# Four plain tiles and one block product in the first third of a feed-forward layer, instead of six plain tiles

## The chip, the cores and the metric

The kernel runs on one core of one Trainium2 chip. The metric is the device time of one execution in microseconds. It is given as the median of three runs. One more execution was taken with the hardware profiler, and its time is given beside its span.

## The reference, cut to what matters

One decoder layer in float32 on 512 tokens of width 1024: a SwiGLU feed-forward at half weight, a mixer (state-space heads and differential attention), cross-attention into 256 memory positions, a second feed-forward and a last norm. The change lies in the first feed-forward alone:

```
def swiglu(h, w_in, w_out):
    gate, up = jnp.split(h @ w_in, 2, axis=-1)
    return (jax.nn.silu(gate) * up) @ w_out

x = x + 0.5 * swiglu(rms_norm(x, norm_ffn1_w[l]), ffn1_w_in[l], ffn1_w_out[l])
```

`w_in` is 1024 x 5632 and `w_out` is 2816 x 1024. The 2816 inner columns are 22 tiles of 128.

## The kernel before, in words

**Precision.** A float32 product is made of three products of rounded parts: each operand is split into a high part (h) and the rest (l), and hh, hl and lh are added. A weight tile of 128 x 1024 is loaded raw (`wr`), ScalarE makes its high part (`wh`), and VectorE the low part (`wl`), lines 155 and 156. There are six buffers for `wr` and three each for `wh` and `wl`.

**Tiles of the first feed-forward** (`ffn1`). The 22 inner tiles are worked in thirds of 6, 8 and 8 (`THIRDS`). In each third the tiles come first, and then `out_blocks` multiplies them with their part of `w_out` and adds the result to x. A tile can be made in two ways.

- **Plain** (`proj`): gate (`pg`) and up (`pu`) each take 8 blocks of the inner dimension times 3 products, that is 24 matmuls 128x512. `gated` turns the two into the tile `th`: VectorE multiplies `pg` by the row of the norm (line 426), ScalarE applies silu (427), and VectorE multiplies with `pu` into `th` (429, 430, 432).
- **By blocks** (`quad`): two tiles at once by the scheme of Strassen and Winograd, which has seven block products instead of eight. Each block product is 24 matmuls 128x256 (line 240). The seven go, in this order, into `qa` (block 11), `qe` (S1), `qb` (S2), `qa` (12), `qb` (S3), `qe` (S4), `qb` (22). Each needs its own weights: five blocks or sums of blocks are loaded, two of the sums are added up by the DMA queue of GpSimd (line 248), and two more by VectorE (lines 294 and 297). ScalarE copies `qa` into `qb` between the first and the third product (line 289).

The block scheme needs sums of blocks of its input: `block_sums` makes them from x, in four pairs of rows, as S1 to S4 in the parts `s31h`, `s31l`, `s24h` and `s24l` (each pair: `fe`, `fo`, four rows 128x256 and two low parts on VectorE). They are used by all block products of the first feed-forward.

**Before**, `NPLAIN` is 6: the first third is made of six plain tiles. The first two (`ffn_first`, tiles `pa`) use weights that arrive with x. The other four are a loop of four steps, and the block sums are made beside it: pairs 0 and 1 in its first step, pair 2 in its second, pair 3 in its third. The second and third thirds have four `quad`s each.

**Accumulators.** Plain tiles, block products and half of the accumulators of `out_blocks` draw from one pool of four PSUM buffers (`accp`), in turn: a fifth tile takes the buffer of the first, when the last reader of the first is done.

**What sets the order.** SyncE and GpSimd issue in the order in which the program is written (`manual_schedule`). Code that runs beside a dense stage is put in by a small planner (`Order`), which counts TensorE's time in microseconds. On TensorE, VectorE and ScalarE a list scheduler puts the instructions in order when the kernel is built, by its own estimate of when inputs are there. On the chip each engine works down its list in order, so an instruction that is not ready holds up all that stand behind it.

**x by token.** `out_blocks` updates x by token, so `by_token` (line 495) loads x again in the other layout into the same buffers, in eight loads on GpSimd's queue, once the block sums have read the old contents. `out_blocks` asks for its first weights ahead of time (`next(out)`), and the sums of its blocks are added up on GpSimd's queue (line 1316 before) or by VectorE (1326, 1367). Its accumulators are `oa`, `oe` and `ob`, and line 1307 adds them to x.

Of the kernel before, what the change touches and what calls it, by code (L numbers as in the profile page):

```python
# [22 lines left out]
MEM = 256  # L23
EPS = 1e-6

NPLAIN = 6

THIRDS = ((0, 6), (6, 8), (14, 8))
THIRDS2 = ((0, 6), (6, 8), (14, 8))
# [71 lines left out]
def body(tc, a, dbg=None):  # L101
# [17 lines left out]
    def s2(s, dt=F32, shape=(P, T)):  # L119
        if math.prod(shape[1:]) <= T // 2:  # L120
            return sp.tile(list(shape), dt, tag="s1", name=nm(s), bufs=NHALF)
        return sp.tile(list(shape), dt, tag="s2", name=nm(s))

    def s4(s):
        return sp.tile([P, 4, T // 2], F32, tag=s, name=nm(s), bufs=1)

    def small(s, n, bufs=None):
        return tiny.tile([P, n], F32, tag=s, name=nm(s), bufs=bufs)

    def acc(s, shape=(P, T)):  # L130
        return acc_p.tile(list(shape), F32, tag="acc", name=nm(s))
# [10 lines left out]
    od = Order()  # L142
# [29 lines left out]
    def load_w(src, n=D):  # L172
        raw = wp.tile([P, n], F32, tag="wr", name=nm("wr"), bufs=6)
        nc.sync.dma_start(raw, src)
        hi = wp.tile([P, n], R32, tag="wh", name=nm("wh"))
        lo = wp.tile([P, n], R32, tag="wl", name=nm("wl"))
        with ExitStack() as after:
            for i in start:
                after.enter_context(tc.issue_after(i))
            recent[:] = [i.ins for i in split_into(hi, lo, raw)]  # L180
        return hi, lo

    @contextmanager
    def behind(ins):
        with ExitStack() as after:
            for i in ins:
                after.enter_context(tc.issue_after(i))
            yield
# [29 lines left out]
    def block_sums(k0, gain, blocks):  # L218

        fe, fo = s2("fe"), s2("fo")  # L220
        V.tensor_scalar(fe, x[k0], par[:, gain + k0 : gain + k0 + 1], None, ALU.mult)
        V.tensor_scalar(fo, x[k0 + 1], par[:, gain + k0 + 1 : gain + k0 + 2], None, ALU.mult)
        return blocks | sums_of(fe[:, :H], fe[:, H:], fo[:, H:], fo[:, :H])

    def of_halves(even, odd):
        lo, hi = slice(0, H), slice(H, T)
        return {"11": hl(even, lo), "12": hl(odd, lo), "22": hl(odd, hi)}
# [90 lines left out]
    def proj(ps, w, xs, ks=None):  # L318
        n = len(xs)
        for k in ks or range(n):  # L320
            mm3(ps, w, xs[k], k == 0, k == n - 1, wc=slice(k * P, (k + 1) * P))
            yield
# [101 lines left out]
    def gated(pg, pu, row, th, odd):  # L424
        gate = s2("gate")
        V.tensor_tensor(gate, pg, row, ALU.mult)
        S.activation(gate, gate, AF.Silu)
        if odd:
            V.tensor_tensor(th[:, 3], pu[:, :H], gate[:, :H], ALU.mult)
            V.tensor_tensor(th[:, 2], pu[:, H:], gate[:, H:], ALU.mult)  # L430
        else:
            V.tensor_tensor(th[:, 0:2], halves(pu), halves(gate), ALU.mult)

    def ffn_quads(xs, wq, st, nq, made, places, sums=None, fresh=False, prime=None):

        for q in range(nq):
            for out in quad(xs, next(wq), next(sums) if sums else None, fresh and q == 0):
                if out is None:
                    yield
            gs, us = out  # L440
            if prime and q == nq - 1:
                next(prime)
            gate, th = s4("gate"), s4("th")
            for i in range(2):
                row = st.row[:, None, i * H : (i + 1) * H].to_broadcast([P, 2, H])
                V.tensor_tensor(gate[:, 2 * i : 2 * i + 2], halves(gs[i]), row, ALU.mult)
            S.activation(gate, gate, AF.Silu)
            for i in range(2):
                V.tensor_tensor(th[:, places[i]], halves(us[i]), gate[:, 2 * i : 2 * i + 2], ALU.mult)
            made(th)  # L450
            yield
# [3 lines left out]
    def block_tiles(g, n, tied=False):  # L455
        def steps(th, blocks, apart):
            b11 = [s2("g11" + p_, R32, (P, H)) for p_ in "hl"]
            split_into(*b11, th[:, 0])
            blocks["11"] = tuple(b11)
            yield apart  # L460
            for sums in sums_in_steps(*(th[:, i] for i in range(4)), pair=(th[:, 0:2], th[:, 1:3])):
                blocks |= sums or {}
                yield apart
            raw = split("g", th[:, 2:4].rearrange("p a b -> p (a b)"))
            lo, hi = slice(0, H), slice(H, T)
            blocks |= {"22": hl(raw, lo), "12": hl(raw, hi)}

        def made(th):
            g.append({})
            if len(g) < n:  # L470
                od.spawn(steps(th, g[-1], 2.9), 2.9)
            else:
                with behind(list(recent) if tied else []):
                    for _ in steps(th, g[-1], 0.0):
                        pass
        return made

    def ffn_first(h, wa):

        ps = [acc("pa"), aux("pa"), acc("pa"), aux("pa")]  # L480
        for k in range(KT):
            for n in range(4):
                mm3(ps[n], wa[k], h[k], k == 0, k == KT - 1, wc=slice(n * P, (n + 1) * P))
            yield
        yield ps[0], ps[2]
        yield ps[1], ps[3]

    def ffn1(h, wa, at_out, each, done):
        xs = []
        wq, plain = iter(a["f1q"]), a["f1i"]  # L490
        col4, ncol4 = small("col4", 4, bufs=1), small("ncol4", 4, bufs=1)

        def by_token():
            for k in (6, 7, 0, 1, 4, 5, 2, 3):
                G.dma_start(x[k], a["xt"][k])
                yield 0.5

        for ti, (_, nf) in enumerate(THIRDS):
            g = []
            nq = nf // 2  # L500
            made = block_tiles(g, nq, True)
            out = out_blocks(a[f"f1b{ti}"], None, g, col4, ncol4, each if ti == len(THIRDS) - 1 else None, n=nq)
            if ti == 0:
                th, f = s4("th"), 0
                for ps in ffn_first(h, wa):
                    if ps is None:
                        yield
                    else:
                        gated(*ps, st1.row, th, f)
                        f += 1  # L510
                made(th)
                V.tensor_scalar(col4, st1.col, 0.5, None, ALU.mult)
                V.tensor_scalar(ncol4, st1.col, -0.5, None, ALU.mult)
                for n in range(NPLAIN - 2):
                    for i in ((0, 1), (2,), (3,), ())[n]:
                        blocks = of_halves(h[2 * i], h[2 * i + 1])
                        b11 = tuple(s2("h11" + p_, R32, (P, H)) for p_ in "hl")
                        with behind(start):
                            for to, of in zip(b11, blocks["11"]):
                                S.activation(to, of.bitcast(F32), AF.Copy)  # L520
                        xs.append(block_sums(2 * i, C_FFN1, blocks | {"11": b11}))
                    if n == 3:
                        od.spawn(by_token())
                    pg, pu = acc("pg"), acc("pu")
                    yield from proj(pg, load_w(plain[n][0]), h)
                    yield from proj(pu, load_w(plain[n][1]), h)
                    if n % 2 == 0:
                        th = s4("th")
                    if n == NPLAIN - 3:
                        next(out)  # L530
                    gated(pg, pu, st1.row, th, n % 2)
                    if n % 2:
                        made(th)
                h.clear()
                nq -= NPLAIN // 2
            yield from ffn_quads(xs, wq, st1, nq, made, BY_BLOCK, prime=out)
            at_out(ti)
            if ti == len(THIRDS) - 1:
                xs.clear()
            yield from out  # L540
        done()
        banks = [acc, aux, acc, aux]
        yield from turn(1, banks)
        yield from turn(0, banks)
# [923 lines left out]
def layout(i):  # L1468
# [12 lines left out]
    for n, s in (("1", "ffn1"), ("2", "ffn2")):  # L1481
        wi = tiles(i[f"{s}_w_in"][0]).reshape(2 * NF, P, KT // 2, 2, P)
        f0 = NPLAIN if n == "1" else 0

# [5 lines left out]
        if n == "1":  # L1490
            d["f1i"] = wi.reshape(2, NF, P, D)[:, 2:NPLAIN].swapaxes(0, 1).copy()
        wo = i[f"{s}_w_out"][0]
# [48 lines left out]
```

## Time and profile before

| | |
|---|---|
| median of three runs | 1319.59 us (1316.08, 1319.59, 1319.67) |
| profiled execution | 1317.81 us |
| its span (first to last instruction) | 1315.9 us |
| TensorE matmul busy | 1289.6 us, 98% |
| VectorE busy | 984.2 us, 75% |
| ScalarE busy | 706.4 us, 54% |
| GpSimd busy | 129.2 us, 10% |
| granted TensorE clock, mean | 0.997 |

A row of the timeline has the start in us from the span's start, how long it took, the engine and the line, what is written and read, and in brackets how long the engine had been idle before it and what ended that. Matmuls are pipelined, so a row's duration is longer than the distance from one start to the next; the distance is what they cost. The same holds for VectorE, to a smaller extent. PE stands for TensorE, DVE for VectorE, ACT for ScalarE, POOL for GpSimd and SP for SyncE.

### The profile page before, as it was taken

What the parts mean: (1) busy time and instruction counts of PE and PEld (TensorE: products, weight loads), DVE (VectorE), ACT (ScalarE), POOL (GpSimd) and SP (SyncE); (2) the same over time, 40 slices, a digit from 0 to 9 for tenths busy, and PEclk for the clock granted to TensorE, in tenths of its full rate; (3) what the DMA queues carried; (4) which work ended last, traced back from release to release, by engine and by line L of the source; (5) the groups of instructions that cost most, each with busy time, mean ns of one, the idle gap of its engine ahead of it and who ended that gap; (6) DMA issues with size and microseconds to landing.
All of it is one profiled execution on the core that took longest, in us unless ns stands there. A gap on an engine that the chain in (4) does not pass through costs nothing.

```text
span 1315.9 us, 20140 instructions
## 1 busy us (share of the span) xinstructions
PE 1289.6 (98%) x7724; PEld 1124.8 (85%) x7724; DVE 984.2 (75%) x1564; ACT 706.4 (54%) x1192; POOL 129.2 (10%) x151
## 2 busy tenths in 40 slices
PE   9999999999999999999999999999999999999996
PEld 7889998998887778777788877888889999989995
DVE  7987888788775676557867786645678878877786
ACT  6544564565754464346645465434465646555564
POOL 0201001001010011111003022020001000000001
PEclk9999999999999999999999999999999999999998
DMA  7377768776994434763465548683239775556652
GB/s 274 120 192 190 205 183 218 217 200 168 285 294 145 135 67 124 255 178 105 93 187 175 170 132 241 193 224 123 66 101 268 211 231 187 182 192 186 193 195 81
DMA packets 69615, 236.33 MB, mean 180 GB/s; under 512 B 8256, under 2 KB 9760, under 8 KB 69168
## 3 DMA queue, kind: packets, MB, share of 16 engines
q1 hardware_dynamic: 53200, 181.11, 40.2%
q0 software_dynamic: 13520, 46.72, 19.2%
q10 hardware_dynamic: 2800, 7.23, 1.6%
q8 instruction: 60, 0.98, 0.3%
q14 instruction: 35, 0.29, 0.1%
HBM read 232.87 MB, written 50.91 MB: 216 GB/s over the span
## 4 chain that ended last, share of the span: by engine, by line
PE 57%; issue 11%; DVE 4%; ACT 2%; POOL 1%; DMA 1%; POOLq 0%; ACTq 0%; DVEq 0%
PE pm L146 10%; PE qb L240 8%; PE qe L240 5%; PE pxbc L146 5%; PE qa L240 5%; PE pcq L146 3%; PE pz L146 3%; PE ob L1296 3%; PE oa L1296 2%; PE oe L1296 2%; PE pq L146 2%; PE pcv L146 1%; PE pv L146 1%; PE pk L146 1%; DVE wl L156 1%
## 5 line engine op out<-in xcount | busy, mean ns | idle before, releaser
L155 ACT ACTIVATE wh<-wr 128x1024 fp32r<-128x1024 f32 (+1 forms) x329 | 334.3, 1019 | 359.8 <-issue 65.1
L156 DVE TENSOR_TENSOR wl<-wr,wh 128x1024 fp32r<-128x1024 f32 (+1 forms) x329 | 385.5, 1175 | 141.3 <-ACT wh L155 138.3
L774 ACT ACTIVATE ec<-ec,mn 128x512 f32<-128x512 f32 (+3 forms) x64 | 35.4, 554 | 33.8 <-DVE mn L773 33.7
L146 PE MATMUL pxbc<-hnh,wh 128*128 128x512 f32 x128 | 52.6, 411 | 0.0
L146 PE MATMUL pxbc<-hnh,wl 128*128 128x512 f32 x128 | 50.3, 393 | 0.0
L146 PE MATMUL pxbc<-hnl,wh 128*128 128x512 f32 x128 | 50.2, 392 | 0.0
L240 PE MATMUL qb<-s31h,wh 128*128 128x256 f32 x152 | 43.2, 284 | 3.2 <-ACT u L299 3.2
L240 PE MATMUL qe<-s31h,wl 128*128 128x256 f32 x152 | 43.2, 284 | 0.6 <-DVE wl L156 0.6
L240 PE MATMUL qb<-s24h,wl 128*128 128x256 f32 x152 | 43.1, 284 | 0.5 <-DVE wl L156 0.5
L240 PE MATMUL qa<-h11h,wh 128*128 128x256 f32 x152 | 43.1, 283 | 0.0
L240 PE MATMUL qe<-s24h,wl 128*128 128x256 f32 x152 | 43.0, 283 | 0.0
L240 PE MATMUL qb<-hmh,wh 128*128 128x256 f32 x152 | 43.0, 283 | 0.0
L240 PE MATMUL qb<-hmh,wl 128*128 128x256 f32 x152 | 43.0, 283 | 0.0
L240 PE MATMUL qe<-s24l,wh 128*128 128x256 f32 x152 | 43.0, 283 | 0.0
L240 PE MATMUL qe<-s24h,wh 128*128 128x256 f32 x152 | 43.0, 283 | 0.0
L240 PE MATMUL qa<-h11h,wl 128*128 128x256 f32 x152 | 43.0, 283 | 0.0
L240 PE MATMUL qa<-hmh,wh 128*128 128x256 f32 x152 | 43.0, 283 | 0.0
L240 PE MATMUL qa<-hml,wh 128*128 128x256 f32 x152 | 43.0, 283 | 0.0
L240 PE MATMUL qb<-hml,wh 128*128 128x256 f32 x152 | 43.0, 283 | 0.0
L240 PE MATMUL qb<-s24h,wh 128*128 128x256 f32 x152 | 43.0, 283 | 0.0
L240 PE MATMUL qa<-h11l,wh 128*128 128x256 f32 x152 | 43.0, 283 | 0.0
L240 PE MATMUL qb<-s24l,wh 128*128 128x256 f32 x152 | 43.0, 283 | 0.0
(449 smaller groups left out, 4173.6 us busy)
## 6 DMA issues: line engine op xcount, KB each, us to landing
wr<-in_f2q SPq DMA_DIRECT2D x44, 512.0 KB, 4.5
wr<-in_f1q SPq DMA_DIRECT2D x40, 512.0 KB, 4.2
wr<-in_f1b SPq DMA_DIRECT2D x30, 512.0 KB, 4.5
isum<-in_f2q SPq DMA_DIRECT2D x22, 512.0 KB, 6.0
wr<-isum SPq DMA_DIRECT2D x22, 512.0 KB, 4.2
wsum<-in_f2b SPq DMA_DIRECT2D x20, 512.0 KB, 6.7
wr<-wsum SPq DMA_DIRECT2D x20, 512.0 KB, 4.4
wr<-in_f1q POOLq DMA_DIRECT2D x16, 512.0 KB, 5.9
```

Source lines behind the costliest of these rows:

```text
L146: newest_mm[:] = [nc.tensor.matmul(out, w, x, start=start, stop=stop).ins]
L155: S.activation(hi, src, AF.Copy),
L156: V.tensor_tensor(lo, src, hi.bitcast(F32), ALU.subtract),
L240: newest_mm[:] = [nc.tensor.matmul(out, a_[:, wc], b_, start=first and f == 0 and kp == 0 and j == 0, stop=kp == n - 1 and j == 2, skip_gr ...
L774: S.activation(ec[:, :n], ec[:, :n], AF.Exp, bias=mn, scale=-1.0, accum_out=sm[c][:, i : i + 1])
L1296: newest_mm[:] = [nc.tensor.matmul(ps, a_[:, ts], b_[:, ws], start=first and k == 0 and j == 0, stop=k == n - 1 and j == 2, skip_group_che ...
```

## The change

`NPLAIN` becomes 4. The first third is now two tiles from `ffn_first`, two plain tiles, and one `quad` that makes the fifth and sixth. The loop has two steps, and each makes two pairs of block sums. The loads of x by token are asked for behind the loop. The early request of `out_blocks` (`next(out)`) was in the loop's last step but one; it is now made at the end of the `quad`. The weights of the tiles concerned are laid out as blocks instead of plain tiles.

```
-NPLAIN = 6
+NPLAIN = 4
...
                 for n in range(NPLAIN - 2):
-                    for i in ((0, 1), (2,), (3,), ())[n]:
+                    for i in ((0, 1), (2, 3))[n]:
...
-                    if n == 3:
-                        od.spawn(by_token())
...
-                    if n == NPLAIN - 3:
-                        next(out)
                     gated(pg, pu, st1.row, th, n % 2)
...
                 h.clear()
+                od.spawn(by_token())
                 nq -= NPLAIN // 2
             yield from ffn_quads(xs, wq, st1, nq, made, BY_BLOCK, prime=out)
```

Line numbers behind the change are lower by 3 from `by_token` on. Beyond the first third and its `out_blocks` the order on every engine is as it was, but for one matmul named below. Three places show what moves.

**VectorE, between the first two plain tiles and what follows.** Before, these are the last rows up to the product of `pu` and its gate that ends the reading of the first `pu`. `fe`, `fo` and `s` are block sums, `gl` belongs to the tiles from `ffn_first`; the number behind a name tells one tile from another.

```order
L156 TENSOR_TENSOR wl_700<-wr_697,wh_699 128x1024
L210 TENSOR_TENSOR s_120_555<-s_119_554,fe_550 128x256
L601 TENSOR_REDUCE lsum_934<-lamp_933 128x1
L211 TENSOR_TENSOR s_120_555<-s_120_555,fo_551 128x256
L156 TENSOR_TENSOR s31l_561<-s_119_554,s31h_560 128x512
L156 TENSOR_TENSOR s24l_565<-s_120_555,s24h_564 128x512
L156 TENSOR_TENSOR gl_589<-th_284,gh_588 128x512
L426 TENSOR_TENSOR gate_634<-pg_568,row_405 128x512
L432 TENSOR_TENSOR th_541<-pu_463,gate_542 128x512
```

Now the rows up to the same product are these:

```order
L156 TENSOR_TENSOR wl_749<-wr_663,wh_748 128x1024
L210 TENSOR_TENSOR s_130_577<-s_129_576,fe_572 128x256
L297 TENSOR_TENSOR wr_663<-wr_663,wr_668 128x1024
L211 TENSOR_TENSOR s_130_577<-s_130_577,fo_573 128x256
L156 TENSOR_TENSOR s31l_583<-s_129_576,s31h_582 128x512
L156 TENSOR_TENSOR wl_790<-wr_668,wh_789 128x1024
L156 TENSOR_TENSOR s24l_587<-s_130_577,s24h_586 128x512
L598 TENSOR_REDUCE lsum_1028<-lamp_1027 128x1
L156 TENSOR_TENSOR gl_611<-th_284,gh_610 128x512
L426 TENSOR_TENSOR gate_656<-pg_590,row_405 128x512
L432 TENSOR_TENSOR th_541<-pu_463,gate_542 128x512
```

Between `gate_542`, the gate of the first plain tile, and its product `th_541<-pu_463,gate_542` stood 12 rows before, and there stand 25 now: two pairs of block sums instead of one, and five rows 128x1024 of the quad's weights (three `wl`, and the additions of lines 294 and 297) instead of one.

**TensorE, from the quad's first product to its second.** `pg_462`, `pu_463`, `pg_590`, `pu_591` were the four tiles before it in the pool of four, `qa_673`, `qe_674` and `qb_675` follow, so `qe_674` takes the buffer of `pu_463`.

```order
L240 MATMUL qa_673<-h11h_568,wl_677 128x256
L1343 MATMUL ob_957<-ones_r 128x512
L240 MATMUL qe_674<-s31h_432,wh_680 128x256 [waits DVE_49,Activation_49]
L240 MATMUL qe_674<-s31l_433,wh_680 128x256
L240 MATMUL qe_674<-s31h_432,wl_681 128x256
```

Before, plain matmuls stood here. The count of VectorE's rows for which the first matmul of `qe_674` waits is 95, and the 95th row is `th_541<-pu_463,gate_542`. The matmul from `ones_r` clears an accumulator of `out_blocks`; before it stood at the head of `out_blocks`.

**VectorE, in `out_blocks` of the first third, around the update of x from `oa`.** Before, the low parts of the weights for the next product stand ahead of the update (`wl_1004` is needed by its third matmul):

```order
L156 TENSOR_TENSOR wl_1004<-wr_1000,wh_1003 128x1024
L156 TENSOR_TENSOR wl_1027<-wr_1023,wh_1026 128x512
L1307 SCALAR_TENSOR_TENSOR x_79<-oa_858,col_59_282,x_79 128x512
L1307 SCALAR_TENSOR_TENSOR x_83<-oa_859,col_59_282,x_83 128x512
L156 TENSOR_TENSOR wl_1041<-wr_1038,wh_1040 128x1024
```

Now they stand behind it:

```order
L1304 SCALAR_TENSOR_TENSOR x_79<-oa_952,col_59_282,x_79 128x512
L1304 SCALAR_TENSOR_TENSOR x_83<-oa_953,col_59_282,x_83 128x512
L156 TENSOR_TENSOR wl_1098<-wr_1094,wh_1097 128x1024
L156 TENSOR_TENSOR wl_1121<-wr_1117,wh_1120 128x512
L156 TENSOR_TENSOR wl_1135<-wr_1132,wh_1134 128x1024
```

On TensorE four matmuls of that product which need no `wl` are put first, and then the clearing matmul of the next third, which before stood in the first quad behind:

```order
L1293 MATMUL ob_956<-wh_1097,s31h_515 128x512
L1293 MATMUL ob_956<-wh_1097,s31l_516 128x512
L1293 MATMUL ob_957<-wh_1097,s31h_515 128x512
L1293 MATMUL ob_957<-wh_1097,s31l_516 128x512
L1343 MATMUL ob_2206<-ones_r 128x512
L1293 MATMUL ob_956<-wl_1098,s31h_515 128x512
```

On SyncE the first quad of the second third asks for its second raw tile when `wl_1121` has freed a buffer; before, it was `wl_1027`, the row behind `wl_1004` above.

## The prediction

> **What bounds the kernel now.** I read the busy shares first, then the stretches around the change, then the rows.
>
> ```profile
> PE 1289.6 (98%) x7724; PEld 1124.8 (85%) x7724; DVE 984.2 (75%) x1564; ACT 706.4 (54%) x1192; POOL 129.2 (10%) x151
> ...
> PE 57%; issue 11%; DVE 4%; ACT 2%; POOL 1%; DMA 1%; POOLq 0%; ACTq 0%; DVEq 0%
> ```
>
> TensorE is busy 98% and holds most of the chain that ended last. Engines differ by stage, though, and the averages hide that. The stretches here (columns: stretch, length, busy us of PE, weight load, DVE, ACT, POOL, clock, DMA share, GB/s):
>
> ```profile
> 40.00:50.00 10.00, 10.00 (x46) 8.29 (x45) 9.57 (x21) 5.79 (x8) 0.00 (x0) 1.00 0.21 68
> 50.00:60.00 10.00, 10.00 (x46) 8.29 (x45) 9.90 (x21) 5.40 (x8) 4.83 (x9) 1.00 0.41 120
> 60.00:70.00 10.00, 10.00 (x46) 8.29 (x45) 7.07 (x13) 3.58 (x6) 2.19 (x3) 1.00 0.96 287
> ```
>
> TensorE has no gap here, so its work sets the time. But VectorE, at 75% over the whole span, is full from 40 to 60 us: 9.57 and 9.90 of 10. It merely isn't waited for. Whatever the change adds to VectorE in this stretch can become the wait that ends last.
>
> **TensorE's own work.** Two plain tiles and the clearing matmul behind them:
>
> ```profile
> 51.70 0.39 PE L146 MATMUL pg<-hmh,wh 128*128 128x512 f32 x1
> ...
> 57.15 0.39 PE L146 MATMUL pu<-hmh,wh 128*128 128x512 f32 x1
> ...
> 73.47 0.40 PE L1346 MATMUL ob<-ones_r 128*128 128x512 f32 x1
> 73.70 0.40 PE L1296 MATMUL oa<-wh,g11h 128*128 128x512 f32 x1
> ```
>
> From 51.70 to 73.47 stand 4 x 24 matmuls: 21.77 us, 0.227 each. A quad without waits, from its first row to the next quad's:
>
> ```profile
> 124.30 0.28 PE L240 MATMUL qa<-h11h,wh 128*128 128x256 f32 x1
> ...
> 144.46 0.28 PE L240 MATMUL qa<-h11h,wh 128*128 128x256 f32 x1
> ```
>
> 20.16 us for 168 matmuls: 0.12 each, 2.88 a product. So the change takes **1.6 us** of work from TensorE. That is all that it can save.
>
> **The wait for the accumulator of the second product.** The quad starts at 51.70, as what stands ahead is unchanged, and its first product ends at 54.58. The second writes `qe`, in the buffer of the first `pu`, and by the order shown it may start when VectorE has done `th<-pu`. When is that? VectorE's rows before, from the gate to that product:
>
> ```profile
> 46.61 0.68 DVE L426 TENSOR_TENSOR gate<-pg,row 128x512 f32<-128x512 f32 x1
> 47.21 0.48 DVE L221 TENSOR_SCALAR fe<-x,par 128x512 f32<-128x512 f32 x1
> 47.60 0.48 DVE L222 TENSOR_SCALAR fo<-x,par 128x512 f32<-128x512 f32 x1
> 48.00 0.42 DVE L206 TENSOR_TENSOR s<-fe 128x256 f32<-128x256 f32 x1
> 48.33 0.42 DVE L207 TENSOR_TENSOR s<-fe,fo 128x256 f32<-128x256 f32 x1
> 48.67 1.22 DVE L156 TENSOR_TENSOR wl<-wr,wh 128x1024 fp32r<-128x1024 f32 x1
> 49.80 0.41 DVE L210 TENSOR_TENSOR s<-s,fe 128x256 f32<-128x256 f32 x1
> 50.14 0.21 DVE L601 TENSOR_REDUCE lsum<-lamp 128x1 f32<-128x64 f32 x1
> 50.27 0.41 DVE L211 TENSOR_TENSOR s<-s,fo 128x256 f32<-128x256 f32 x1
> ...
> 51.99 0.68 DVE L156 TENSOR_TENSOR gl<-th,gh 128x512 fp32r<-128x512 f32 x1
> 52.60 0.68 DVE L426 TENSOR_TENSOR gate<-pg,row 128x512 f32<-128x512 f32 x1
> 53.20 0.68 DVE L432 TENSOR_TENSOR th<-pu,gate 128x512 f32<-128x512 f32 x1
> ...
> 106.37 1.22 DVE L294 TENSOR_TENSOR wr<-wr,wr 128x1024 f32<-128x1024 f32 x1
> ```
>
> Costs are the distances of starts: `fe`, `fo` 0.40; `s` 0.335; 128x512 0.605; small rows 0.13; `wl` 1.13. The additions of the quad have the duration of a `wl` (1.22), so 1.13 too. Before, the product came at 53.20 and the next user of its buffer (the third `pu`, 57.15) didn't wait. Now 25 rows stand between gate and product: 4 x 0.40, 8 x 0.335, 5 x 1.13, six of 128x512 at 0.605, 2 x 0.13: 1.60 + 2.68 + 5.65 + 3.63 + 0.26 = 13.82. The gate itself stays at about 46.6 (three small rows ahead of it go, 0.4 us, but a `wl` there waits for TensorE as before). So the product starts at 47.21 + 13.82 = 61.03 and ends at 61.7. No input is later than VectorE itself: the quad's raw tiles take the place of plain ones in SyncE's list, which are asked for from 10 to 25 us, and `wh` of block 12 needs only the first product's end.
>
> ```profile
> 10.06 15.17 SPq L174 DMA_DIRECT2D wr<-in_f1i  x8
> ```
>
> TensorE thus starts the second product at 61.7 instead of 54.58: **7.1 us** idle, less the clearing matmul, which fits in. The other six take 17.28, and `oa` starts at 79.0 against 73.70: **+5.3**, the saving included. Within the six I see no wait: VectorE is past its heap, the copy `qa` to `qb` stands on ScalarE behind a silu that needs the gate just ahead of `th`, so it is done by 62.5, two microseconds ahead of its use, and later products need a `wl` each 2.88 us, which took 1.13.
>
> The tail of the quad (gate, silu, `th`, sums) must be ready 5.5 us after its end, when `oa` and `oe` have used up the first two blocks. In the later thirds:
>
> ```profile
> 184.78 0.40 PE L1296 MATMUL oa<-wh,g11h 128*128 128x512 f32 x1
> ...
> 190.73 0.42 DVE L156 TENSOR_TENSOR g11l<-th,g11h 128x256 fp32r<-128x256 f32 x1
> ...
> 308.54 0.40 PE L1296 MATMUL oa<-wh,g11h 128*128 128x512 f32 x1
> ...
> 312.81 0.41 DVE L156 TENSOR_TENSOR g11l<-th,g11h 128x256 fp32r<-128x256 f32 x1
> ```
>
> From the end of the quad to the end of `g11l` it took 6.4 and 4.7 us. I put 0, at most 1.
>
> **The third product of `out_blocks`.** Its `wl` now stands behind the two updates of x from `oa`.
>
> ```profile
> 88.52 1.81 DVE L156 TENSOR_TENSOR wl<-wr,wh 128x1024 fp32r<-128x1024 f32 x2
> 90.25 1.40 DVE L1307 SCALAR_TENSOR_TENSOR x<-oa,col,x 128x512 f32<-128x512 f32 x2
> ...
> 90.04 0.39 PE L1296 MATMUL ob<-wh,s31h 128*128 128x512 f32 x1
> ```
>
> The second update can't start before 0.2 after `ob`'s first matmul; with what stands ahead some 0.4. Then 0.66 for it and 1.22 for `wl`: 2.3 after `ob`'s start. TensorE has four matmuls and the moved clearing one: 1.13. It waits **1.2** (bounds 0.9 and 1.5). The clearing matmul is saved later, where it stood: a wash.
>
> **The first quad of the second third.** It waits already, for weights that land late:
>
> ```profile
> 106.39 0.39 PE L240 MATMUL qe<-s31h,wl 128*128 128x256 f32 x1 [0.61 <-DVE wl L156]
> 110.05 0.39 PE L240 MATMUL qb<-s24h,wl 128*128 128x256 f32 x1 [0.54 <-DVE wl L156]
> ```
>
> The request on SyncE comes behind the `wl` just treated and one of 128x512. Against `ob`'s start both end 2.6 us later than before; TensorE itself loses 1.4 of that (wait and clearing matmul), so 1.2 is added to a wait that exists: **+1.1**, bounds 0 and 1.4. From there on the order is as before, TensorE is full again, and nothing gives time back.
>
> Sum so far: 5.3 + 1.2 + 1.1 = **+7.6**.
>
> **What TensorE's pace is after 7 us of idleness.** No wait that long is in the trace. The nearest rows:
>
> ```profile
> 2.39 3.35 PE L342 MATMUL init<-ones_r 128*128 128x512 f32 x7 [2.39 <-ACT ones_r L340]
> 6.08 0.80 PE L146 MATMUL pa<-hmh,wah 128*128 128x512 f32 x1 [0.33 <-ACT wah L155]
> ...
> 7.06 0.40 PE L146 MATMUL pa<-hmh,wal 128*128 128x512 f32 x1
> ...
> 335.15 0.51 PE L1296 MATMUL oe<-wh,s24h 128*128 128x512 f32 x1 [2.38 <-ACT wh L155]
> 335.49 0.40 PE L1296 MATMUL ob<-wl,s31h 128*128 128x512 f32 x1
> ```
>
> At the program's start the seven `init` took 3.35 us where 6 x 0.227 + 0.39 = 1.75 is usual: 1.6 lost. Counted to 7.06, where the usual pace begins, 4.67 - 0.33 - 9 x 0.227 = 2.3 is lost. After a wait of 2.4 us the loss is 0.1. So the price lies between 0.1 and 2.3. An idle time of 7 us is nearer to a start from rest than to 2.4 us, so I take the middle of the two upper values, **+1.9**. [...] The rows at the start agree with half pace, while the profile's clock column prints 1.00 for 2 to 4 us; so the pace is to be read from the distances.
>
> Sum: 7.6 + 1.9 = **+9.5**. The profiled execution took 1317.81 (span 1315.9), which makes 1327.3. The median of the runs is 1319.59, 1.8 above it; the mean of all four times is 1318.3, which gives 1327.8. I say **1327.5**.
>
> **The rivals.**
> - *The clock stays up.* Then +7.6: 1325.4 to 1325.9. For it speaks 335.15, against it the start. 0.25.
> - *The tail is later.* Eight loads of x go out on GpSimd's queue at 53 to 57, just ahead of the additions for `out_blocks`, and the last third of those weights waits for buffers that the quad holds. If they land late, `oa`'s second part or the third product waits 2 to 3 us more: about 1330. Against it: these loads stood ahead of the same additions before, and TensorE had no gap. 0.10.
> - *Faster: the wait is covered.* Four buffers in turn let VectorE empty one while TensorE fills the next, as the third `pu` at 57.15 shows. [...] If `th<-pu` were done by 54.58, TensorE would run through and keep its 1.6: 1316.2, or 1316.7 against the mean. It decides at 7.4 us for the 25 rows behind the gate; they need 13.8, and each has a row of before. 0.03.
> - *The change doesn't do what it says.* The order shows 168 matmuls in place of 96 and the same names behind it. I give it nothing of its own; 0.02 goes to a result near zero from causes that I don't see.
>
> **How the numbers follow.** Forecast 0.60, clock stays 0.25, later tail 0.10, faster 0.03, near zero 0.02. The forecast's own range, from the bounds of its terms, is 1325 to 1329.5. To take in the second and half of the third case the range goes from 1323 to 1331. About 0.3%, 4 us, is what a measurement of this kernel can tell from no change. Forecast, slow tail and steady clock all lie above 1323.6: slower 0.93, same 0.04, faster 0.03.
>
> **What would show it.** Right: a `qe` row at about 61.7 whose wait of some 7 us ends with VectorE's `th`; matmuls 128x256 at up to twice 0.12 us apart for the next 3 to 5 us; `oa` 7 us later than 73.70; a wait at the third product of `out_blocks`. Wrong: a `th<-pu` row well before 61 (then my count of VectorE's rows is off), full pace right behind the wait, or time given back in the second third, where TensorE waits 1.3 us for weights now.

## The result, and the profile after

The changed kernel takes 1331.99 us, the median of four runs (1330.70 to 1332.96), the kernel before 1319.63 on the same chip (four runs, 1316.08 to 1320.78). The ratio is 1.0103, interval 1.008 to 1.0125: slower by some 11 to 16 us. The direction was as forecast, and so was the long wait inside the block product; the size was not: 1327.5 was forecast, and 1331 was the range's upper end. The profiled execution took 1332.96, span 1331.2.

The page after, engines and chain:

```profile
PE 1293.4 (97%) x7796; PEld 1131.1 (85%) x7796; DVE 991.8 (75%) x1570; ACT 710.3 (53%) x1197; POOL 130.8 (10%) x153
...
PE 56%; issue 11%; DVE 4%; ACT 2%; POOL 1%; DMA 1%; POOLq 0%; ACTq 0%; DVEq 0%
```

These two lines hardly differ from those of before: an average over 1300 us doesn't show a loss of 12. The stretches do (columns as in the prediction):

```profile
50.00:60.00 10.00, 6.61 (x41) 5.71 (x39) 10.00 (x19) 4.64 (x7) 4.59 (x9) 1.00 0.32 102
60.00:70.00 10.00, 6.47 (x37) 6.50 (x38) 5.67 (x13) 3.12 (x6) 0.62 (x1) 0.66 0.68 189
```

From 50 to 60 VectorE is busy for all 10.00 us and TensorE for 6.61: the bound has passed to VectorE. From 60 to 70 the clock column falls to 0.66. TensorE's rows there:

```profile
56.22 0.40 PE L1343 MATMUL ob<-ones_r 128*128 128x512 f32 x1
63.53 0.55 PE L240 MATMUL qe<-s31h,wh 128*128 128x256 f32 x1 [6.92 <-DVE lamp L597]
63.88 0.42 PE L240 MATMUL qe<-s31l,wh 128*128 128x256 f32 x1
64.10 0.42 PE L240 MATMUL qe<-s31h,wl 128*128 128x256 f32 x1
...
68.14 0.28 PE L240 MATMUL qe<-s31h,wh 128*128 128x256 f32 x1
68.26 0.28 PE L240 MATMUL qe<-s31l,wh 128*128 128x256 f32 x1
...
82.89 0.40 PE L1293 MATMUL oa<-wh,g11h 128*128 128x512 f32 x1
```

And VectorE's, from the gate to the product that was waited for:

```profile
48.24 0.68 DVE L426 TENSOR_TENSOR gate<-pg,row 128x512 f32<-128x512 f32 x1
...
61.50 0.68 DVE L156 TENSOR_TENSOR gl<-th,gh 128x512 fp32r<-128x512 f32 x1
62.10 0.68 DVE L426 TENSOR_TENSOR gate<-pg,row 128x512 f32<-128x512 f32 x1
62.70 0.68 DVE L432 TENSOR_TENSOR th<-pu,gate 128x512 f32<-128x512 f32 x1
```

The second product waits 6.92 us and starts when `th<-pu` is done (63.38); the releaser printed, `lamp`, is merely the row that starts at that moment. Then the matmuls stand 0.214 apart instead of 0.12 until 68.14.

Where the 15.15 us between the two profiled executions (1332.96 and 1317.81) lie, by TensorE's starts in both traces:

| place | us |
|---|---|
| up to the gate of the first plain tile (29.93 before, 31.55 after) | +1.6 |
| gate to `oa`: work -1.6, idle +7.1, slow pace +2.1 | +7.6 |
| `oa` to the third product of `out_blocks` | +0.2 |
| third product | +1.6 |
| first block product of the second third, to its fourth product | +2.9 |
| `out_blocks` of the second third | +0.6 |
| all the rest, to the end | +0.6 |

The third product and the block product behind it, where the forecast was furthest off:

```profile
99.44 0.39 PE L1293 MATMUL ob<-wh,s31h 128*128 128x512 f32 x1
...
101.86 0.50 PE L1293 MATMUL ob<-wl,s31h 128*128 128x512 f32 x1 [1.12 <-DVE wl L156]
...
116.07 0.28 PE L240 MATMUL qa<-h11h,wl 128*128 128x256 f32 x1
118.52 0.39 PE L240 MATMUL qe<-s31h,wh 128*128 128x256 f32 x1 [2.17 <-ACT wh L155]
118.75 0.28 PE L240 MATMUL qe<-s31l,wh 128*128 128x256 f32 x1
119.78 0.58 PE L240 MATMUL qe<-s31h,wl 128*128 128x256 f32 x1 [0.76 <-DVE wl L156]
120.16 0.42 PE L240 MATMUL qe<-s31h,wh 128*128 128x256 f32 x1
...
122.72 0.29 PE L240 MATMUL qe<-s31h,wh 128*128 128x256 f32 x1
...
126.68 0.28 PE L240 MATMUL qa<-hmh,wh 128*128 128x256 f32 x1
```

After two waits in a row, of 2.2 and 0.8 us, the matmuls are 0.21 apart again, from 119.78 to 122.72. The weights waited for are loaded by SyncE's queue, and GpSimd's queue adds the second block to them:

```profile
102.44 0.33 SPq L246 DMA_DIRECT2D wr<-in_f1q  x1
...
108.25 0.85 POOL L248 DMA_DIRECT2D wr<-in_f1q  x1 [14.92 <-DVE wl L156]
...
117.42 1.06 ACT L155 ACTIVATE wh<-wr 128x1024 fp32r<-128x1024 f32 x1 [7.14 <-DMA wr<-in_f1q]
```

The same places before, and the fourth product of that block product:

```profile
90.36 0.33 SPq L246 DMA_DIRECT2D wr<-in_f1q  x1
...
95.72 0.85 POOL L248 DMA_DIRECT2D wr<-in_f1q  x1 [12.50 <-DVE x L1307]
...
104.02 1.06 ACT L155 ACTIVATE wh<-wr 128x1024 fp32r<-128x1024 f32 x1 [4.78 <-DMA wr<-in_f1q]
...
112.78 0.28 PE L240 MATMUL qa<-hmh,wh 128*128 128x256 f32 x1
```

From SyncE's request to ScalarE's use 15.0 us pass, before 13.7; 9.2 and 8.3 of them follow GpSimd's request for the addition.

### The profile page after: what moved, and what is told of

It is laid out like the page before. It is cut to its first block, busy times and chain, and to the rows that moved or that the text cites. A ratio compares the mean times of both kernels' runs of the same rounds, so it can differ in the third digit from the quotient of the medians.

```text
span 1331.2 us, 20300 instructions
## 1 busy us (share of the span) xinstructions
PE 1293.4 (97%) x7796; PEld 1131.1 (85%) x7796; DVE 991.8 (75%) x1570; ACT 710.3 (53%) x1197; POOL 130.8 (10%) x153
## 4 chain that ended last, share of the span: by engine, by line
PE 56%; issue 11%; DVE 4%; ACT 2%; POOL 1%; DMA 1%; POOLq 0%; ACTq 0%; DVEq 0%
PE pm L146 10%; PE qb L240 8%; PE qe L240 5%; PE pxbc L146 5%; PE qa L240 5%; PE pcq L146 3%; PE ob L1293 3%; PE pz L146 3%; PE oa L1293 2%; PE oe L1293 2%; PE pq L146 2%; PE pcv L146 1%; PE pv L146 1%; PE pk L146 1%; DVE wl L156 1%
## 5 line engine op out<-in xcount | busy, mean ns | idle before, releaser
L156 DVE TENSOR_TENSOR wl<-wr,wh 128x1024 fp32r<-128x1024 f32 (+1 forms) x332 | 389.6, 1177 | 149.9 <-ACT wh L155 146.1
L240 PE MATMUL qe<-s31h,wh 128*128 128x256 f32 x160 | 47.0, 294 | 9.1 <-DVE lamp L597 6.9
L240 PE MATMUL qe<-s31h,wl 128*128 128x256 f32 x160 | 47.0, 294 | 0.8 <-DVE wl L156 0.8
L240 PE MATMUL qe<-s31l,wh 128*128 128x256 f32 x160 | 46.7, 292 | 0.0
L240 PE MATMUL qb<-s31h,wl 128*128 128x256 f32 x160 | 45.3, 283 | 0.0
```

Source lines behind the costliest of these rows:

```text
L156: V.tensor_tensor(lo, src, hi.bitcast(F32), ALU.subtract),
L240: newest_mm[:] = [nc.tensor.matmul(out, a_[:, wc], b_, start=first and f == 0 and kp == 0 and j == 0, stop=kp == n - 1 and j == 2, skip_gr ...
```

## The experiments

All times are medians; each ratio is to the kernel before, run beside it on the same chip. "Stretch" is the time from the start of the third product of `out_blocks` to the fourth product of the first block product of the second third: 22.7 us before, 27.2 after, and 25.0 by the forecast.

### What the second product waits for: e1, e2, e4

```diff
-        e_ps = acc("qe")
-        b_ps = acc("qb")
+        e_ps = (aux if spare else acc)("qe")
+        b_ps = (aux if spare else acc)("qb")
```

> The changed kernel, but in the first third the accumulators qe and qb of the block product come from the other PSUM pool, so that neither takes a buffer that VectorE still has to read. Theory A (the accumulator is what the second product waits for, and all else is ready): qe follows qa without a gap, the wait of 6.9 us and the half pace behind it (2.1 us) both go, about 9 us: 1323 us. Theory B (VectorE's whole list is late, the accumulator is only the first thing that shows it): qe starts early, but waits inside the quad for the low parts of the last pair of block sums, which end at 61.5 in the changed kernel, and for weights treated behind them; about 4 us of waits stay, in pieces under 2 us, and the gain is 3 to 6 us: 1326 to 1329.

This kernel leaves out the matmul that clears the new buffer of `qb`, so the copy of `qa` in it is not added to, and the result is not the layer's; e8 has that matmul.

Measured: 1323.93, ratio 1.0033 (1.002 to 1.0045). `qe` follows `qa` at once. The time is near theory A's and below theory B's range, but the waits inside the quad are those of theory B:

```profile
PE qb L240 <- ACT u L299: 1.9, 1, 1.9
...
PE qe L240 <- DVE wl L156: 0.8, 1, 0.8
PE qe L240 <- DVE s31l L156: 0.6, 1, 0.6
PE qb L240 <- DVE wl L156: 0.5, 1, 0.5
PE qe L240 <- ACT s31h L155: 0.5, 1, 0.5
```

(Columns: who, for whom, total us, times, longest. The 0.8 belongs to the second third.) From `qa` to `oa` it takes 26.0 us against 29.6 after, so 3.6 are won here; the rest of the 8 us is a stretch of 24.7 instead of 27.2, and the start. Only the first of these is the edit's for certain: the stretch and the start also vary without it (e5).

```diff
-                        th = s4("th")
+                        th = s4("gate")
```

> The changed kernel, but the tile th of the second pair lies in the buffer of the quads' gate instead of the one buffer that all th share. Nothing else is edited. Theory A (VectorE's rows stand in the way one by one, as the prediction counted them): the place of the product does not depend on that buffer, and the time stays at 1332. Theory B (the product stands behind 25 rows because its th has to wait for the last reader of the th before): the product comes up to a few rows behind its gate, near 51 us, and qe starts at once. What is next late is the buffer of qb, whose gate is still near 62 us: the wait moves there and is 2 to 4 us shorter, the half pace may go: 1328 to 1331.

Measured: 1330.67, ratio 1.0087 (1.0072 to 1.0102). VectorE:

```profile
46.39 0.68 DVE L426 TENSOR_TENSOR gate<-pg,row 128x512 f32<-128x512 f32 x1
...
48.11 0.68 DVE L432 TENSOR_TENSOR gate<-pu,gate 128x512 f32<-128x512 f32 x1
...
60.40 0.69 DVE L156 TENSOR_TENSOR gl<-th,gh 128x512 fp32r<-128x512 f32 x1
61.00 0.69 DVE L426 TENSOR_TENSOR gate<-pg,row 128x512 f32<-128x512 f32 x1
```

The product stands four rows behind its gate instead of 26. So its late place came from the one buffer of `th`: the new tile had to wait for `gl<-th`, the last reader of the old one. But TensorE then waits 1.3 us for the copy `qa` to `qb`, 1.1 and 0.5 for sums and weights and 2.2 for `u`, with half pace between (the profile's mean clock is 0.992, after 0.994), and `qa` to `oa` takes 30.6. One late buffer hid what was late behind it.

```diff
-                    for i in ((0, 1), (2,), (3,), ())[n]:
+                    for i in ((0, 1), (2, 3), (), ())[n]:
```

> The kernel before, with six plain tiles, of which one part of the change is made: the block sums in two pairs, in the first two steps of the loop. No block product in the first third. Theory A (the wait needs both, the early sums and the five low parts and two additions of the block product on VectorE): the third pu waits at most 1 us for the buffer of the first, and the time is 1319 to 1321. Theory B (the sums in two pairs alone make VectorE late): the third pu waits 4 us or more, and with the half pace behind it the time is 1324 or more.

Measured: 1319.34, ratio 1.0004 (0.9995 to 1.0013). Theory A, with a short wait at the third `pu`:

```profile
58.28 0.47 PE L146 MATMUL pu<-hmh,wh 128*128 128x512 f32 x1 [0.67 <-DVE gate L426]
```

The wait ends with the gate of the second plain tile, one row ahead of `th<-pu`; that it is a wait for the buffer of the first `pu` is not shown. The sums in two pairs cost nothing where six plain tiles follow. In front of the quad they would not be free: `th<-pu` ends at 58.7 here, and the quad asks for that buffer at 54.6. An estimate from these rows is that some 4 us of the wait of 7 come without the quad's weights and additions on VectorE, and that these make the other 3 (`qe` starts at 61.9 in e5).

### TensorE's pace: e3, e12

```diff
+            if fill:
+                ps = aux("fill")
+                for _ in range(fill):
+                    with behind(list(newest_mm)):
+                        newest_mm[:] = [nc.tensor.matmul(ps, ones_r, ones_r[:, None, :].to_broadcast([P, 4, P]), start=True, stop=True).ins]
```

> The changed kernel with 28 more matmuls 128x512 of ones, written into a spare PSUM buffer that nobody reads, between the first and the second block product, 6.35 us at 0.227 each, so that TensorE works while it waits. Theory A (the half pace after the wait comes from TensorE's idleness): qe still starts about 7 us late, but its matmuls go at 0.12 from the first one on, and the 2.1 us are saved: 1330. Theory B (the slow matmuls come from something else, for example weights or sums that trickle in): the 24 matmuls of qe keep their 5.0 us, and the time stays at 1332 or grows.

Measured: 1326.40, ratio 1.0055 (1.004 to 1.007).

```profile
54.35 5.88 PE L294 MATMUL fill<-ones_r 128*128 128x512 f32 x25
...
61.67 0.36 PE L240 MATMUL qe<-s31h,wh 128*128 128x256 f32 x1 [0.53 <-DVE lamp L603]
61.86 0.28 PE L240 MATMUL qe<-s31l,wh 128*128 128x256 f32 x1
61.98 0.28 PE L240 MATMUL qe<-s31h,wl 128*128 128x256 f32 x1
```

The same wait for the same product, but full pace from the first matmul on: 2.94 us for the 24 instead of 4.97. So of the 7.9 us between the two profiled executions 2.0 lie here. `oa` starts at 79.00, where the prediction put it before its term for the pace. Here too the stretch was 24.6, 2.6 less than after, and the start was 1.9 earlier; neither is shown to come from the filling.

The same filling, of 8 matmuls, only at the wait for the second weights:

> The changed kernel with 8 more matmuls 128x512 of ones, 1.8 us, between the first and the second block product of the second third, where TensorE waits 1.5 to 2.2 us for weights, and nowhere else. Theory A (the half pace of the 24 matmuls behind that wait, 1.5 us, comes from the wait of 2.2 us together with that of 0.8 behind it): with the first filled the pace stays at 0.12 and 1.5 us are saved, less what the filling is longer than the wait, 1330. Theory B (the slow matmuls there are owed to the operands): the same 5.3 us for the 24 matmuls, 1332.

Measured: 1330.67, ratio 1.0098 (1.0076 to 1.012).

```profile
113.51 2.02 PE L294 MATMUL fill<-ones_r 128*128 128x512 f32 x8
115.37 0.28 PE L240 MATMUL qe<-s31h,wh 128*128 128x256 f32 x1
115.49 0.28 PE L240 MATMUL qe<-s31l,wh 128*128 128x256 f32 x1
```

Theory A for the pace: the 24 matmuls took 2.88 us. The stretch is 24.4. The time as a whole is not clear of the changed kernel's: the four runs lie between 1328.4 and 1334.7.

### Again, and the order of the rows in out_blocks: e5, e6, e7, e10

> The changed kernel once more without an edit, for a second profile of it. In the first one two things were not forecast: the gate of the first plain tile started at 31.55 instead of 29.93 us, and the first block product of the second third waited 2.2 us for its second weights, which e1 and e3 did for 0.3 only. Theory A (both are chance, from the phase of the clock at the start and from transfers that vary): the first gate starts near 29.9, the second weights wait is under 1 us, and the profiled time is 2 to 4 us under 1333. Theory B (both belong to the kernel): 31.5 and 2.2 us again.

Measured: 1331.17, ratio 1.0097 (1.0076 to 1.0118); the profiled execution 1330.46. The first gate starts at 29.93, exactly as before: the 1.6 us of the start were chance. (In all profiles it lies between 29.3 and 31.6. TensorE's full pace began at 10.1 us in the first profile, at 7.1 here and at 7.0 before.) The slow `qe` took 4.36 instead of 4.97. The wait for the second weights was 1.5 us, the stretch 26.5: that part belongs to the kernel, and varies. Much later, at 345 us, a single wait of 2.9 us in `out_blocks` of the third third was followed by half pace here (clock 0.50 from 345.02 to 348.43), and the pace cost 1.3 us more than behind the same wait before (2.4 us, the row at 335.15 in the prediction); in the first profile it cost nothing more.

```diff
+        w3 = weights(sums[1], parts[0]) if here and n == 3 else None
+        with behind(recent[1:] if w3 else []):
             for t in range(2):
                 update(t, 0, a_ps[t])
-        yield from product(b_ps, sums[1], S3)
+        yield from product(b_ps, sums[1], S3, ready=w3)
```

> The changed kernel, but in the first third VectorE treats the first weights of the third product of out_blocks ahead of the two updates of x from oa, as in the kernel before. Theory A (the order of these rows makes the wait there, and the later requests behind it make the wait of the first block product of the second third): 1.3 us fewer at the third product and 1 to 2.5 us fewer at the block product, 1328 to 1330. Theory B (VectorE is late as a whole there, so the next weights are late instead): the wait moves to the next product, and the time stays within 0.5 us of 1332.

Measured: 1331.04, ratio 1.0098 (1.0081 to 1.0114). Theory B: the third product took 4.37 us instead of 5.72, the next one 0.6 more, and the wait for the second weights grew to 2.7; the stretch is 27.25, after it was 27.24. So the third product's wait was no cost of its own as long as the later wait is there: what ends the stretch is when those weights arrive.

For e7 the split of these weights goes behind the updates in the kernel before:

> The kernel before, with that one order taken from the changed kernel: in the first third the first weights of the third product of out_blocks stand behind the two updates of x from oa. Nothing else is changed. Theory A (the prediction's terms hold by themselves): a wait of 1.2 us at the third product and 1.1 us more at the first block product of the second third, 2.3 us together: 1321.5. Theory B (the rows are done early enough where VectorE is not late from the block product ahead): the third product waits less than 0.5 us and the time stays at 1319 to 1320.

Measured: 1321.68, ratio 1.0025 (1.0013 to 1.0038). The third product hardly waits, as TensorE's list has four matmuls of the next one between; the stretch is 24.2 instead of 22.7, 0.3 of it there and 0.9 at the second weights, the clearing matmul left out at both. The time is theory A's, the place is not; and the profiled execution, at 1318.78, was the fastest of the ten.

For e10 the same edit as in e6 is made for all weights of the last three products:

> The changed kernel, in which only the order of out_blocks in the first third is that of the kernel before: all weights of the third, sixth and seventh product ahead of the updates of x. e6 moved one of the six only. Theory A (the requests for the second third stand behind these rows, so the whole row order has to go back): the third product's wait (1.5) goes, and the second weights of the first block product are asked for 1.3 us earlier and waited for less than 1 us, with no half pace: 3 to 4.5 us less, 1327 to 1328. Theory B (as in e6 the wait only moves): 1331.

Measured: 1329.98, ratio 1.009 (1.007 to 1.0111), stretch 25.3. The wait for the weights fell to 0.8, but with the 0.8 behind it the pace still broke (24 matmuls in 5.44). The time is not clear of the changed kernel's: two of the four runs took 1327.8, two 1332.1 and 1332.7.

### The second weights: e13

```diff
-            t, m3, m2, m7 = raw_w(b12, b11), raw_w(b22), raw_w(b21), raw_w(b12, b22)
+            t = raw_w(b12) if vadd else raw_w(b12, b11)
+            if vadd:
+                V.tensor_tensor(t, t, m1, ALU.add)
+            m3, m2, m7 = raw_w(b22), raw_w(b21), raw_w(b12, b22)
```

> The changed kernel with one edit: in the first block product of the second third the sum of two weight blocks is made by VectorE from the block that is loaded for the first product anyway, in place of a second transfer that adds on GpSimd's queue. Theory A (the wait there is that for the transfer and the adding transfer one behind the other, 12.1 to 16.1 us from request to ScalarE in the runs so far): the sum is ready some 5 us earlier, the wait for ScalarE's wh (2.2) and the half pace of the next 24 matmuls (1.5) go: qe starts right behind qa, and the time is 1327 to 1329. Theory B (the requests and VectorE itself are late): VectorE's new row of 1.13 us makes the wait longer or only moves it: 1331 or more.

Measured: 1325.25, ratio 1.005 (1.0036 to 1.0063): some 6 us less than the changed kernel by one addition, 4.0 to 4.7 of them in the stretch (against e5 and the first profile).

```profile
105.75 1.22 DVE L272 TENSOR_TENSOR wr<-wr,wr 128x1024 f32<-128x1024 f32 x1 [0.73 <-DMA wr<-in_f1q]
...
113.38 0.28 PE L240 MATMUL qa<-h11h,wl 128*128 128x256 f32 x1
113.50 0.28 PE L240 MATMUL qe<-s31h,wh 128*128 128x256 f32 x1
```

The sum is ready 6.5 us ahead of its use, and `qe` follows `qa` without a gap at full pace. The stretch is 22.5, less than before. The transfer with the adding transfer behind it was the wait. (The edit also takes a transfer of 512 KB away; what less traffic alone would bring is not shown.) The third product still takes 5.7 here, and with the later wait gone this counts: e14, which has neither, has a stretch of 21.4.

### Towards a version without the waits: e8, e9, e11, e14, e15

e8 adds these to e1 and e2:

```diff
+        if spare:
+            nc.tensor.matmul(b_ps, ones_r, ones_r[:, None, :].to_broadcast([P, 4, P]), start=True, stop=True)
...
-        V.tensor_scalar(fe, x[k0], par[:, gain + k0 : gain + k0 + 1], None, ALU.mult)
+            S.activation(fe, x[k0], AF.Copy, scale=par[:, gain + k0 : gain + k0 + 1])
```

> The changed kernel with three edits: qe and qb of the first block product from the other PSUM pool (with a clearing matmul for qb, which e1 left out, so that there the copy of qa was not added to), th of the second pair in the gate's buffer, and fe and fo of the block sums made by ScalarE instead of VectorE, eight rows of 0.40 us fewer. Theory A (VectorE's amount of work up to 62 us is what is left of the wait in e1): the waits in qe and the first qb of e1, 0.8, 0.4, 0.7 and 0.5 us, go, that of 2.2 us at the second qb for ScalarE's copy u stays: oa starts 2 us earlier than in e1, at 75.5, and the time is 1321 to 1322. Theory B (the copy u and what stands ahead of it on ScalarE is the end of another chain that only gets longer with ScalarE's new work): the wait at u grows by as much, and the time stays at 1324 or more.

Measured: 1324.83, ratio 1.0047 (1.0029 to 1.0065). In the quad theory A: `qa` to `oa` 22.7 us, only the wait at `u` (1.9) is left. The stretch behind took 27.4 in this profile, which gives that back, so the time is not theory A's. The three edits were made together; what the lighter VectorE alone brings is not shown.

e11 puts ScalarE's copy `u` ahead of the split that stood before it; e9 restores the order of e10 as well:

> e9 without the order in out_blocks: the edits of e8 and the copy u ahead. Theory A (the copy u stood behind another split on ScalarE): no wait of 2 us at the second qb, oa 2 us earlier than in e8, at 72.1 against the first gate's 29.33 there; everything behind as in e8: 1322 to 1323. Theory B (VectorE's subtraction or the weights of the fifth product are late next): at least 1 us of the 2 comes back there, 1324.

> The edits of e8, and two more: ScalarE's copy u in the block product of the first third ahead of the split that stood before it, and in the first third's out_blocks VectorE treats all weights of the third, sixth and seventh product ahead of the updates of x, in the order of the kernel before. Theory A (the waits of e8, 2.0 us at u, 1.5 at the third product and 3 at the first block product of the second third with its half pace, come from these orders): oa starts at 72.2 or a little later, the third product waits under 0.5, the block product as in the kernel before (1.5): 1317 to 1319, at or just under the kernel before. Theory B (VectorE and the transfers are late as a whole): at least 3 us of waits come back at the next places, 1321 or more.

Measured: e11 1325.87 (1.0062, 1.004 to 1.0083), e9 1323.02 (1.0038, 1.0024 to 1.0052). The wait at `u` is gone, and 0.9 and 1.2 us come back in the next product, at weights of VectorE's. The stretches are 28.9 and 27.0: theory B in both, because the adding transfer is still there (waits of 2.8 and 3.0 us for it).

> All edits of e9 and the one of e13. Theory A: e9 without its wait of 3.0 us for that sum and without the half pace behind it (1.4): 4 to 4.5 us less than e9, 1318 to 1319, level with the kernel before. Theory B: the wait comes back at the third or fifth product of that block product, and 2 us or less are gained: 1321 or more.

Measured: 1317.28, ratio 0.9992 (0.9983 to 1.0001), over 11 runs. Of TensorE's waits in the part concerned one over 0.5 us is left:

```profile
PE qe L244 <- DVE wl L156: 0.9, 1, 0.9
```

The quad in the first third, with its surroundings put right, is level with six plain tiles, not clearly better.

> The kernel before with the edit of e13 alone. Theory A (there the two waits at that place, 0.8 and 0.7 us, end with VectorE's low parts of the sums that come with these transfers): one or both go, 0.8 to 1.6 us less: 1317 to 1318.5 where the kernel before takes 1319. Theory B (VectorE's new row costs what the transfer took): no change within 0.5 us.

Measured: 1317.12, ratio 0.9993 (0.9984 to 1.0002). Both waits of the kernel before at that place are gone (stretch 21.1), but by the interval the gain is not clear of zero. These two are the best versions found.

## Why the prediction was right and wrong, step by step

**TensorE's work, -1.6: right.** The 120 matmuls from 68.50 to 82.89 take 0.12 each.

**The accumulator, 7.1 us: right in place and size, incomplete in its reason.** 61.7 was forecast for the start of `qe`; e3 has 61.67, e5 61.91. The count of VectorE's rows held. But it took the product's place in the list as given. e2 shows why it was there (one buffer of `th`), and e1 and e2 that behind it stood further waits of about the same end: taking one away wins 3.6 us or nothing. That VectorE's work up to 62 us is the real limit fits e8, which lightens it and takes these waits away, but e8 has the edits of e1 and e2 as well.

**The tail of the quad, 0 to 1: right** (0.2). **The third product, 1.2: right in size** (1.4 without the clearing matmul), **but no term of its own** beside the wait behind it, as e6 shows.

**The pace after the wait, 1.9: right, with luck in the size.** Six profiles have this wait of 6.9 us; the loss was 1.5 in four of them (e5 is one), 2.1 in the first and 2.7 in e6. The rival "the clock stays up" was forecast at 1325.4 to 1325.9; e3, in whose profile TensorE's clock doesn't fall before the program's end (its mean is 0.998, before 0.997), gave 1326.4.

**The first block product of the second third, +1.1 with bounds 0 and 1.4: this step failed.** It measured 3.1 after and 2.4 in e5, clearing matmul left out. Two things in it were wrong. The path of the second weights was taken over from before as a fixed length, 13.7 us from SyncE's request to ScalarE; in the first fourteen profiles it took 12.1 to 16.1, and before lies in the middle. (Why it varies stays open: the order of the requests was the same in most of them, and the DMA engines were 0.85 to 1.05 busy on that way in all.) And the slow pace was charged for the wait of 7 us only; the row at 335.15, a single wait of 2.4 us, was read as "0.1 after a short wait". That was one draw: at the same place nine of all 17 profiles lost 1.5 to 1.8 us. Here the waits of 2.2 and 0.8 us together cost 1.5 more. e13 takes that transfer away and the loss with it.

**Given nothing, and found:** the start, +1.6 in the profiled execution, is chance by e5. Without it the steps up to the fourth product of that block product make 12.3 us in the first profile and 10.9 in e5; the medians differ by 12.4. And what comes behind was forecast as unchanged; but the pace behind the single wait in `out_blocks` of the third third cost 1.3 us more in e5. Half pace follows it in nine of the thirteen profiles with the block product in the first third and in none of the four without, which may be chance.

The rival of a later tail had a late transfer as its mechanism, and with 1330 came nearest; it put the lateness at `out_blocks` itself, not behind it. That its number came nearest is luck.

## What to carry to other kernels

When a full engine is handed more work, look not only for how many rows stand ahead of the one that is waited for, but for what put it behind them (here one buffer's last reader), and for what would be late next. A wait that already exists is a place without slack: there the spread of a transfer counts in full, and its bounds belong into the range. Where traces show pace lost behind waits, price short waits that lie close together as one (here 2.2 and 0.8 us together cost 1.5 us more), and put a lone wait of about 2 us at both its prices, here 0.1 to 0.2 and 1.5 to 1.8 us: one row of one profile doesn't show which.

## What the runs showed of the hardware

- In the changed kernel's profile TensorE's clock falls to half twice before the program's end: from 61.29 to 68.11 us, which begins in the wait of 6.92 us, and from 119.31 to 122.73, which begins in the second of the waits of 2.17 and 0.76 us. Before, the clock column reads 1.00 from 10 to 1307 us of 1315.9. What sets when it falls and when it comes back is not shown.
- A lone wait has both outcomes. Below (columns as in the prediction), the stretch behind the two waits at the second weights in the changed kernel; the stretch behind the single wait of 2.9 us in `out_blocks` of the third third in e5; and the stretch around the end of the same wait before, of 2.38 us.

```profile
119.31:122.73 3.42, 2.95 (x14) 2.95 (x15) 2.20 (x3) 1.65 (x2) 0.70 (x1) 0.50 0.60 97
...
345.02:348.43 3.41, 2.83 (x7) 2.26 (x8) 3.27 (x5) 1.93 (x5) 0.00 (x0) 0.50 0.93 240
...
334.70:338.12 3.42, 2.97 (x13) 2.44 (x14) 3.42 (x5) 1.81 (x5) 0.00 (x0) 1.00 0.81 194
```

- Lost beyond the waits, over the next 24 matmuls, at the second weights: 1.5 to 1.7 us for 1.6 to 3.1 us and then 0.9 us of standing still, two matmuls between (after, e2, e5, e6, e8, e9), but 2.6 in e11 (2.9 and 0.6); 0.2 for 0.3 and 0.9 (e1, e3); for about 1.0 and 0.9 once 0.2 (e7) and once 1.6 (e10). A single wait of 1.9 us cost 0.1 (e8, at `u`), the same one behind four others 1.6 (e1). The pace behind the single wait in `out_blocks` of the third third, over 30 matmuls, cost 1.5 to 1.8 in nine profiles (1.9 to 3.0 us long) and 0.1 to 0.2 in eight (1.1 to 2.5 us).
- With matmuls of ones into a spare PSUM buffer through the wait, the 24 matmuls behind it took 2.94 us (e3, against 4.97 in the changed kernel) and 2.88 (e12).
- The clock column shows the fall inside the kernel (0.50 from 61.29 to 68.11 us), but prints 1.00 for the program's first 10 us, where the matmuls 128x512 stand 0.43 apart in the changed kernel's profile: its clock record begins at 10.1 us only.

```profile
8.00:10.00 2.00, 2.00 (x7) 1.52 (x6) 1.99 (x4) 1.84 (x4) 0.00 (x0) 1.00 0.99 354
...
61.29:68.11 6.82, 4.58 (x21) 4.61 (x22) 4.10 (x11) 1.45 (x3) 0.00 (x0) 0.50 0.84 223
```
